# A hybrid decoder layer: modulation by pairs of feature tiles, with w_cond held in TensorE in float32

## The chip, the cores and the metric

The kernel runs on one core of a Trainium2 chip. The core has a matrix engine (TensorE, PE in the profile), three engines for elementwise work (VectorE or DVE, ScalarE or ACT, GpSimd or POOL), SyncE (SP), which issues most loads and stores, and 16 DMA engines that carry them. Every engine works through a queue of its own in a fixed order and waits for the others by semaphores. The metric is the device time of one execution in microseconds; less is better.

## The reference

One layer of a decoder with two branches, attention and a state-space model, on 1024 prompt tokens and 8 sample tokens. Only its first two steps matter here: the condition vector `c` of each of nine sequences (one prompt, eight samples) gives a shift and a scale for each of 1024 features, and the modulated input goes through one wide projection.

```python
def _modulate(x, c, w_cond, b_cond):
    mod = c @ w_cond + b_cond
    shift, scale, gate = jnp.split(mod, 3, axis=-1)
    h = x * (1.0 + scale[:, None]) + shift[:, None]
    return h, gate[:, None]

def _project_in(h, w_in):
    z = h @ w_in
    q, k, v, g_att, u, g_ssm, m_att, m_ssm = jnp.split(z, IN_SPLITS, axis=-1)
    ...
```

`c` is (1 + 8) x 1024, `w_cond` is 1024 x 3072 (the gate's third is used at the end of the kernel and is not touched here), `h` is 1032 x 1024, `w_in` is 1024 x 8192. All is float32.

## The kernel before

Features lie along the 128 partitions, so the transposed input `xt` comes as eight tiles of 128 features by 1032 tokens (`xs[t]`). Float32 products are made of faster ones: an operand is split into a high part (rounded, a cast on ScalarE) and a low part (the difference, on VectorE), and three products hi x hi, hi x lo, lo x hi are summed. For the projections the parts of a tile are `ahi` and `alo` (`split_act`), those of a slab of w_in (512 KB, 128 output features) `whi` and `wlo` (`Weights.emit`; one buffer for the slab as it comes, two for its parts).

A projection job (`gemm`) takes one slab and writes 128 output features in three column chunks: 8 feature tiles x 3 chunks x 3 products, 72 matmuls of 128x128 by 344 columns. The first four jobs are q, k, v and the gate of head pair 0. `Stream` hands out their matmuls: `begin` opens jobs, `head` takes matmuls of the opened ones ahead of time, `drain` and `weave` run the rest, the latter between the steps of the attention.

`modulate` (L241) runs at the very start. For the first half of the features (tiles 0 to 3), then for the second, it forms rows of `mod`: `c`, split and packed into 128 columns (`csplit`), is held in TensorE, and the split w_cond (`wchi`, `wclo`, in pieces of 256 rows by 512 columns, 16 loads in all) moves past it (`cond_product`, L346). The result, 9 rows of high and 9 of low parts, is copied out (`modr`, L270), and `features` (L277) turns it into columns by 8 small matmuls with a selector `sel`, in float32, of 128 columns held and 9 moving (each float32 matmul of the program stands as two in the trace: 16 there). Then `md` gets the bias (L281, L282), each tile is modulated, tiles 1, 3, 5, 7 on ScalarE (L285), 0, 2, 4, 6 on VectorE (L287), the sample columns by L288 and L289, and split (L236, L237). During the second half, `head(FILL)` puts five projection matmuls of jobs 0 and 1 behind each piece, up to half of each job.

The tables of the state-space model (`ssm_tables`, a generator that `modulate` advances by `next(tabs)`) are woven in: small loads (a_re, a_im, log_dt, mult), some 45 steps of 128x32 on VectorE (L383 to L413), four large steps on GpSimd (L418 to L427) with rounding steps on VectorE between them (L379, L425), two sines on ScalarE (L428, L429), and products. The order on VectorE, ScalarE, GpSimd and SyncE is set when the program is built, by a scheduler with priorities (`high_priority` moves a step ahead); on TensorE it is the order in which the code is written.

After job 0, the q columns are copied (`Attention.evac`, L581), split on ScalarE (L586) and GpSimd (L587); after job 1 the k columns likewise, their parts are turned to the other half of the partitions by DMAs (L612, L614), and the first scores (L661) multiply them.

Of the kernel before, what the change touches and what calls it, by code (L numbers as in the profile page):

```python
# [9 lines left out]
F32 = mybir.dt.float32  # L10
F32R = mybir.dt.float32r
I32 = mybir.dt.int32
AF = mybir.ActivationFunctionType
ALU = mybir.AluOpType
# [3 lines left out]
NP, NS, NT = 1024, 8, 1032  # L18
NC3, CW = 3, 344
KT = 8  # L20
# [11 lines left out]
EDGE = 2  # L32
ORDER = {3: (3, 0, 1, 2), 0: (0,), 2: (0, 2, 1), 1: (1, 0)}
HURRY = 400
WCB = 8
ONACT = (1, 3, 5, 7)
FILL = 5
WQ = "pps"
QUEUES = "sasssasss"
PACE = 155  # L40
# [2 lines left out]
GS = "v"  # L43
LATE = 5.0
AHEAD = 2
FILL2 = 10
DRAIN = 1.6
EARLY = 2
TWO_PI = 6.283185307179586
MULT = [float(j) for j in range(9)] + [8.0 * j for j in range(16)] + [128.0 * j for j in range(8)]  # L50
NM = len(MULT)
# [33 lines left out]
def blk(i, w=128):  # L85
    return slice(w * i, w * i + w)
# [61 lines left out]
class Stream:  # L148
# [24 lines left out]
    def head(self, n):  # L173

        for job in self.begun:
            while n and job[1] < KT * 9 // 2:
                next(job[0])
                job[1] += 1
                n -= 1
                self.left -= MM  # L180
                self.clock += MM

# [59 lines left out]
def modulate(k, sp, ps, io, tabs):  # L242


    nc, S = k.nc, k.stream
    PE, ACT, DVE, SP = nc.tensor, nc.scalar, nc.vector, nc.sync
    ct = sp.tile([128, KT, 9], F32, name="ct", bufs=1)
    SP.dma_start(ct, io["ct"])
    cc = split_c(k, sp, ct)
    todo = deque((q, 1024 * s + 512 * half) for half in range(2) for s in range(2) for q in range(4))  # L250
    ahead, xs = deque(), {}

    def load():
        if todo:
            q, c0 = todo.popleft()
            ahead.append(cond_load(k, sp, io, q, c0, WCB))

    def load_x(half):
        for t in range(4 * half, 4 * half + 4):
            xs[t] = sp.tile([128, NT], F32, tag="xt", bufs=5, name="xt")  # L260
            SP.dma_start(xs[t], io["xt"][t])

    def rows(fill):
        ps_ = ps.tile([128, 512], F32, tag="mod", name="mod")
        for q in range(4):
            cond_product(k, ps_, cc, q, cond_split(k, sp, ahead.popleft(), 2))
            load()
            fill()
        r = sp.tile([64, 512], F32, tag="modr", bufs=2, name="modr")
        ACT.copy(r, ps_[0:64])  # L270
        return r

    def features(half, rs):
        pm = ps.tile([128, 512], F32, tag="mod", name="pm")[:, 0:128].rearrange("p (i s n) -> p i s n", i=4, s=2)
        for i in range(4):
            for s in range(2):
                PE.matmul(pm[:, i, s, 0:9], rs[s][:, blk(i)], sel, start=True, stop=True)  # L277
        for i in range(4):
            t = 4 * half + i
            md = sp.tile([128, 2, 9], F32, tag="md", bufs=2, name="md")  # L280
            DVE.tensor_scalar(md[:, 0], pm[:, i, 0, 0:9], bc[:, t:t + 1], None, op0=ALU.add)  # L281
            DVE.tensor_scalar(md[:, 1], pm[:, i, 1, 0:9], bc[:, 8 + t:9 + t], 1.0, op0=ALU.add, op1=ALU.add)  # L282
            x = xs.pop(t)
            if t in ONACT:
                ACT.activation(x[:, 0:NP], x[:, 0:NP], AF.Identity, scale=md[:, 1, 0:1], bias=md[:, 0, 0:1])  # L285
            else:
                DVE.tensor_scalar(x[:, 0:NP], x[:, 0:NP], md[:, 1, 0:1], md[:, 0, 0:1], op0=ALU.mult, op1=ALU.add)  # L287
            DVE.tensor_tensor(x[:, NP:NT], x[:, NP:NT], md[:, 1, 1:9], ALU.mult)  # L288
            DVE.tensor_tensor(x[:, NP:NT], x[:, NP:NT], md[:, 0, 1:9], ALU.add)  # L289
            k.act_h.append(split_act(k, k.hp, x))  # L290

    for n in range(WCB):
        if n == EARLY:
            next(tabs)
        load()
    sel = sp.tile([64, 9], F32, name="sel", bufs=1)
    SP.dma_start(sel, io["sel"])
    bc = sp.tile([128, 16], F32, name="bc", bufs=1)
    SP.dma_start(bc, io["bc"])
    next(tabs)  # L300
    load_x(0)
    k.w.ahead = 2
    k.w.ensure()
    SP.dma_start(k.ident, io["ident"])
    SP.dma_start(k.hb, io["sb_bias"].broadcast_to((128, H)))
    r = [rows(lambda: None) for _ in range(2)]
    features(0, r)
    load_x(1)
    k.w.ahead = 0
    S.begin(2)  # L310
    r = [rows(lambda: S.head(FILL)) for _ in range(2)]
    S.head(FILL2)
    features(1, r)
    S.head(72)
    k.w.ahead = 1


def split_c(k, sp, ct, tag="csplit"):

    nc = k.nc  # L320
    cc = sp.tile([128, KT, 128], F32R, name="csplit", tag=tag, bufs=1)
    nc.vector.memset(cc.bitcast(F32), 0.0)
    nc.vector.tensor_copy(cc[:, :, 0:9], ct)
    nc.vector.tensor_tensor(cc[:, :, 32:41], ct, cc[:, :, 0:9].bitcast(F32), ALU.subtract)
    return cc
# [1394 lines left out]
```

## Time and profile before

| what | value |
|---|---|
| median of 3 runs | 1667.35 us (1664.79 to 1669.0) |
| profiled execution | 1668.55 us, span 1666.5 us |
| TensorE busy | 1497.7 us, 90% of the span |
| VectorE busy | 1265.3 us, 76% |
| ScalarE busy | 754.0 us, 45% |
| GpSimd busy | 895.0 us, 54% |
| mean granted TensorE clock | 0.958 |

The span runs from the first to the last instruction; the execution's own time is about 2 us longer. Busy shares are means over stages that differ: the first 80 us are the modulation, the tables and the first two jobs, then come attention, the state-space branch and the output products. A time in the timeline is counted from the span's start; the second number of a row is the duration of one instruction or of a run of like ones, and a bracket tells the idle time ahead of it and what ended it.

### The profile page before, as it was taken

How to read it: one execution, taken by the hardware profiler on the slowest of the kernel's cores; microseconds unless marked ns; L12 is line 12 of the kernel's file. 1: busy time of each engine (PE TensorE's matmuls, PEld its weight loads, DVE VectorE, ACT ScalarE, POOL GpSimd, SP SyncE). 2: the span in 40 equal slices, each digit the busy share in tenths (PEclk: the TensorE clock that was granted, in tenths of full speed). 3: DMA queues.
4: the chain of work that ended last, by engine and by line, in shares of the span. 5: the costliest groups of instructions: out<-in, count | busy, mean ns of one | idle time of the engine just before them, and what ended most of it. 6: DMA issues, size and time to landing. Idle time of an engine off the chain costs nothing.

```text
span 1666.5 us, 26016 instructions
## 1 busy us (share of the span) xinstructions
PE 1497.7 (90%) x9257; PEld 1423.4 (85%) x9257; DVE 1265.3 (76%) x2342; ACT 754.0 (45%) x1380; POOL 895.0 (54%) x744
## 2 busy tenths in 40 slices
PE   4899899999999999999989898987988869999997
PEld 3799898989898989899978888887878869999885
DVE  8748888888888888872688878978559994544566
ACT  4466666666676666663333333333352222321200
POOL 3437676767676767664456555456336542122154
PEclk8899999999999999999999999889989989999998
DMA  9233333333333333326689888768355576754322
GB/s 333 71 100 82 81 81 81 81 81 81 82 81 82 81 81 81 81 88 205 214 274 292 261 256 266 256 200 233 113 181 172 188 266 240 250 182 150 105 89 89
DMA packets 164125, 258.72 MB, mean 155 GB/s; under 512 B 45049, under 2 KB 106233, under 8 KB 163867
## 3 DMA queue, kind: packets, MB, share of 16 engines
q1 hardware_dynamic: 137945, 163.62, 32.5%
q0 software_dynamic: 23456, 84.95, 15.9%
q10 hardware_dynamic: 2594, 8.49, 1.9%
q8 instruction: 73, 1.20, 0.3%
q14 instruction: 57, 0.47, 0.1%
HBM read 188.38 MB, written 57.86 MB: 148 GB/s over the span
## 4 chain that ended last, share of the span: by engine, by line
PE 41%; DVE 25%; issue 8%; DMA 5%; ACT 4%; POOL 2%; SPq 0%; DVEq 0%; ACTq 0%; POOLq 0%
PE pj L142 26%; PE f L1403 6%; DVE l_t L895 4%; DVE s_sc L837 3%; DVE ke L672 3%; PE o L707 3%; PE tp L690 2%; DMA s_t<-in_cache_k,s_idx 2%; PE z L661 2%; DVE vs L643 2%; DVE be L673 2%; DVE s_t L832 1%; DMA w<-in_w_in 1%; DVE m L1255 1%; DVE ox L716 1%
## 5 line engine op out<-in xcount | busy, mean ns | idle before, releaser
L142 PE MATMUL pj<-ahi,whi 128*128 128x344 f32 x2112 | 700.9, 333 | 56.9 <-ACT u L981 20.4
L142 PE MATMUL pj<-alo,whi 128*128 128x344 f32 x2112 | 691.3, 329 | 10.3 <-DVE alo L1231 5.8
L142 PE MATMUL pj<-ahi,wlo 128*128 128x344 f32 x2112 | 585.0, 329 | 14.2 <-POOL wlo L110 14.2
L142 PEld LDWEIGHTS pj<-ahi,whi 128*128 128x128 f32 x2112 | 410.3, 194 | 65.6 <-ACT u L981 21.4
L142 PEld LDWEIGHTS pj<-alo,whi 128*128 128x128 f32 x2112 | 410.5, 194 | 15.3 <-DVE alo L1231 6.9
L142 PEld LDWEIGHTS pj<-ahi,wlo 128*128 128x128 f32 x2112 | 385.0, 193 | 17.6 <-POOL wlo L110 15.8
L672 DVE TENSOR_TENSOR_SCAN ke<-ke,eye 128x896 f32<-128x896 f32 (+7 forms) x128 | 214.2, 1674 | 81.9 <-ACT ke L662 81.5
L110 POOL TENSOR_TENSOR wlo<-w,whi 128x1024 fp32r<-128x1024 f32 x53 | 134.2, 2532 | 242.7 <-ACT whi L109 242.4
L109 ACT CAST whi<-w 128x1024 fp32r<-128x1024 f32 x90 | 94.9, 1055 | 162.0 <-PE pj L142 111.3
L662 ACT ACTIVATE ke<-z,nhb 128x448 f32<-128x448 f32 (+2 forms) x192 | 112.0, 583 | 82.6 <-PE z L661 79.2
L673 DVE TENSOR_TENSOR be<-be,ke 128x896 f32<-128x896 f32 (+7 forms) x128 | 128.3, 1003 | 11.7 <-DVE ke L672 0.5
L837 DVE SCALAR_TENSOR_TENSOR s_sc<-s_t,s_q,s_sc 128x512 f32<-128x512 f32 x126 | 112.4, 892 | 22.0 <-issue 9.9
L663 ACT ACTIVATE be<-z,hb 128x448 f32<-128x448 f32 (+2 forms) x192 | 110.7, 577 | 0.0
L816 POOL DMA_INDIRECT s_t<-in_cache_k,s_idx x64 | 71.3, 1114 | 39.8 <-issue 12.8
L690 PE MATMUL tp<-ident,be 128*128 128x128 f32 x576 | 89.4, 273 | 0.0
L495 POOL TENSOR_TENSOR pr<-tab 128x256 f32<-128x256 f32 x32 | 31.1, 972 | 102.4 <-DMA tab<-d_tab 98.8
L693 ACT CAST wthi<-tp 128x512 fp32r<-128x512 f32 x96 | 56.6, 590 | 54.7 <-PE tp L690 52.6
L895 DVE SCALAR_TENSOR_TENSOR l_t<-l_t,l_sc 128x128 f32<-128x128 f32 x256 | 78.5, 366 | 2.3 <-DMA l_t<-in_cache_v,l_idx 2.3
L496 POOL TENSOR_TENSOR pt<-tab 128x256 f32<-128x256 f32 x64 | 77.8, 1216 | 3.1
L574 POOL TENSOR_TENSOR sg<-sg,zg 128x1024 f32<-128x1024 f32 x8 | 22.0, 2746 | 99.2 <-ACT sgs L573 99.2
L1525 ACT ACTIVATE gate<-pj 128x344 f32<-128x344 f32 x72 | 33.0, 459 | 92.2 <-PE pj L142 90.1
L661 PE MATMUL z<-kl,qs 128*128 128x448 f32 (+2 forms) x192 | 66.7, 348 | 3.0 <-DMA kl<-kl 3.0
(320 smaller groups left out, 2865.6 us busy)
## 6 DMA issues: line engine op xcount, KB each, us to landing
w<-in_w_in SPq DMA_DIRECT2D x38, 512.0 KB
w<-in_w_in POOLq DMA_DIRECT2D x26, 512.0 KB
wc<-in_w_cond SPq DMA_DIRECT2D x24, 512.0 KB
gst<-d_gg SPq DMA_DIRECT2D x8, 576.0 KB
x<-in_xr SPq DMA_DIRECT2D x9, 512.0 KB
xt<-in_xt SPq DMA_DIRECT2D x8, 516.0 KB
d_ma<-gate SPq DMA_DIRECT2D x8, 516.0 KB
d_mm<-gate SPq DMA_DIRECT2D x8, 516.0 KB
```

The source lines that it names most:

```text
L109: nc.scalar.copy(whi, w32)
L110: self.eng.tensor_tensor(wlo, w32, whi.bitcast(F32), ALU.subtract)
L142: PE.matmul(ps[c], w[:, blk(t)], x[:, cs(c)], start=(t == 0 and i == 0), stop=(t == KT - 1 and i == 2))
L661: nc.tensor.matmul(z[:, 0:wide], st["q", h][:, blk(i)], x[:, s:s + wide], start=j == 0, stop=j == 1)
L662: nc.scalar.activation(ke[:, s:s + cw], z[:, 0:cw], AF.Sigmoid, bias=k.nhb[:, hd:hd + 1], scale=-0.125)
L663: nc.scalar.activation(be[:, s:s + cw], z[:, 0:cw], AF.Sigmoid, bias=k.hb[:, hd:hd + 1], scale=0.125)
L672: nc.vector.tensor_tensor_scan(rev, rev, self.eye[:, NP - n:][:, ::-1], 0.0, ALU.mult, ALU.add)
L673: nc.vector.tensor_tensor(be, be, ke[:, 1:n + 1], ALU.mult)
L690: PE.transpose(tp[:, 2 * order[a] + e], w[e][:, blk(2 * j + a)], k.ident)
L837: DVE.scalar_tensor_tensor(sc, t, q[:, d - d0:d - d0 + 1], sc, op0=ALU.mult, op1=ALU.add)
L895: nc.vector.scalar_tensor_tensor(t[:, d], t[:, d], 1.0, self.sc, op0=ALU.mult, op1=ALU.mult, accum_out=self.acc[:, j, 8 * c + d:8 * c + d ...
L1403: PE.matmul(pp[c], a[:, token(i)], w[:, blk(c, 512)], start=(t == 0 and a is ah and w is wh), stop=(t == KT - 1 and a is al))
```

## The change

Modulation goes by pairs of feature tiles, four of them. w_cond comes in blocks of 512 rows by 256 columns (1 KB rows), four for a pair, and is held in TensorE unsplit, in float32; `c` moves past it with its 9 columns, also unsplit. The product of a pair stands in features by columns at once (`pm`), so `sel`, `csplit`, `wchi`, `wclo` and `modr` go. One VectorE step adds both biases for a pair (`bcs`, with the 1 of 1 + scale in it). All eight tiles are modulated on ScalarE. `head(n)` now brings each opened job up to its n-th matmul: after the small matmuls of pair g, jobs 0 and 1 follow up to 18 g, that is through tiles 0 to 2 g - 1, two tiles behind. The loads are ordered pair by pair, with the first slab of w_in behind pair 0 and the second among those of pair 3; the tables' small loads come behind pair 1.

```diff
 EDGE = 2
 ORDER = {3: (3, 0, 1, 2), 0: (0,), 2: (0, 2, 1), 1: (1, 0)}
 HURRY = 400
-WCB = 8
-ONACT = (1, 3, 5, 7)
-FILL = 5
+WCB = 12
+XTB = 6
 WQ = "pps"
 QUEUES = "sasssasss"
 PACE = 155
...
 GS = "v"
 LATE = 5.0
 AHEAD = 2
-FILL2 = 10
 DRAIN = 1.6
-EARLY = 2
 TWO_PI = 6.283185307179586
 MULT = [float(j) for j in range(9)] + [8.0 * j for j in range(16)] + [128.0 * j for j in range(8)]
 NM = len(MULT)
...
     def head(self, n):
 
         for job in self.begun:
-            while n and job[1] < KT * 9 // 2:
+            while job[1] < n:
                 next(job[0])
                 job[1] += 1
-                n -= 1
                 self.left -= MM
                 self.clock += MM
 
...
     PE, ACT, DVE, SP = nc.tensor, nc.scalar, nc.vector, nc.sync
     ct = sp.tile([128, KT, 9], F32, name="ct", bufs=1)
     SP.dma_start(ct, io["ct"])
-    cc = split_c(k, sp, ct)
-    todo = deque((q, 1024 * s + 512 * half) for half in range(2) for s in range(2) for q in range(4))
-    ahead, xs = deque(), {}
-
-    def load():
-        if todo:
-            q, c0 = todo.popleft()
-            ahead.append(cond_load(k, sp, io, q, c0, WCB))
-
-    def load_x(half):
-        for t in range(4 * half, 4 * half + 4):
-            xs[t] = sp.tile([128, NT], F32, tag="xt", bufs=5, name="xt")
+    ws, xs = {}, {}
+
+    def load(g):
+        for s in range(2):
+            for half in range(2):
+                w = ws[s, half, g] = sp.tile([128, 4, 256], F32, tag="wc", bufs=WCB, name="wc")
+                c0 = 1024 * s + 256 * g
+                SP.dma_start(w, io["w_cond"][512 * half:512 * half + 512, c0:c0 + 256].rearrange("(t p) f -> p t f",
+                                                                                                 p=128))
+        for t in (2 * g, 2 * g + 1):
+            xs[t] = sp.tile([128, NT], F32, tag="xt", bufs=XTB, name="xt")
             SP.dma_start(xs[t], io["xt"][t])
 
-    def rows(fill):
-        ps_ = ps.tile([128, 512], F32, tag="mod", name="mod")
-        for q in range(4):
-            cond_product(k, ps_, cc, q, cond_split(k, sp, ahead.popleft(), 2))
-            load()
-            fill()
-        r = sp.tile([64, 512], F32, tag="modr", bufs=2, name="modr")
-        ACT.copy(r, ps_[0:64])
-        return r
-
-    def features(half, rs):
-        pm = ps.tile([128, 512], F32, tag="mod", name="pm")[:, 0:128].rearrange("p (i s n) -> p i s n", i=4, s=2)
-        for i in range(4):
-            for s in range(2):
-                PE.matmul(pm[:, i, s, 0:9], rs[s][:, blk(i)], sel, start=True, stop=True)
-        for i in range(4):
-            t = 4 * half + i
-            md = sp.tile([128, 2, 9], F32, tag="md", bufs=2, name="md")
-            DVE.tensor_scalar(md[:, 0], pm[:, i, 0, 0:9], bc[:, t:t + 1], None, op0=ALU.add)
-            DVE.tensor_scalar(md[:, 1], pm[:, i, 1, 0:9], bc[:, 8 + t:9 + t], 1.0, op0=ALU.add, op1=ALU.add)
-            x = xs.pop(t)
-            if t in ONACT:
-                ACT.activation(x[:, 0:NP], x[:, 0:NP], AF.Identity, scale=md[:, 1, 0:1], bias=md[:, 0, 0:1])
-            else:
-                DVE.tensor_scalar(x[:, 0:NP], x[:, 0:NP], md[:, 1, 0:1], md[:, 0, 0:1], op0=ALU.mult, op1=ALU.add)
-            DVE.tensor_tensor(x[:, NP:NT], x[:, NP:NT], md[:, 1, 1:9], ALU.mult)
-            DVE.tensor_tensor(x[:, NP:NT], x[:, NP:NT], md[:, 0, 1:9], ALU.add)
+    def features(g):
+        pm = ps.tile([128, 512], F32, tag="mod", name="pm")[:, 0:36].rearrange("p (i s n) -> p i s n", i=2, s=2)
+        for s in range(2):
+            for i in range(2):
+                for t in range(KT):
+                    PE.matmul(pm[:, i, s], ws[s, t // 4, g][:, t % 4, blk(i)], ct[:, t], start=t == 0, stop=t == KT - 1)
+        md = sp.tile([128, 2, 2, 9], F32, tag="md", bufs=2, name="md")
+        with k.tc.high_priority(HURRY):
+            DVE.tensor_tensor(md, pm, bcs[:, 2 * g:2 * g + 2].unsqueeze(3).broadcast_to([128, 2, 2, 9]), ALU.add)
+        for i in range(2):
+            x = xs.pop(2 * g + i)
+            ACT.activation(x[:, 0:NP], x[:, 0:NP], AF.Identity, scale=md[:, i, 1, 0:1], bias=md[:, i, 0, 0:1])
+            DVE.tensor_tensor(x[:, NP:NT], x[:, NP:NT], md[:, i, 1, 1:9], ALU.mult)
+            DVE.tensor_tensor(x[:, NP:NT], x[:, NP:NT], md[:, i, 0, 1:9], ALU.add)
             k.act_h.append(split_act(k, k.hp, x))
 
-    for n in range(WCB):
-        if n == EARLY:
-            next(tabs)
-        load()
-    sel = sp.tile([64, 9], F32, name="sel", bufs=1)
-    SP.dma_start(sel, io["sel"])
+    load(0)
     bc = sp.tile([128, 16], F32, name="bc", bufs=1)
     SP.dma_start(bc, io["bc"])
-    next(tabs)
-    load_x(0)
+    bcs = sp.tile([128, KT, 2], F32, name="bcs", bufs=1)
+    DVE.tensor_copy(bcs[:, :, 0], bc[:, 0:KT])
+    DVE.tensor_scalar(bcs[:, :, 1], bc[:, KT:], 1.0, None, op0=ALU.add)
     k.w.ahead = 2
     k.w.ensure()
+    load(1)
+    next(tabs)
+    load(2)
     SP.dma_start(k.ident, io["ident"])
     SP.dma_start(k.hb, io["sb_bias"].broadcast_to((128, H)))
-    r = [rows(lambda: None) for _ in range(2)]
-    features(0, r)
-    load_x(1)
+    features(0)
+    load(3)
     k.w.ahead = 0
     S.begin(2)
-    r = [rows(lambda: S.head(FILL)) for _ in range(2)]
-    S.head(FILL2)
-    features(1, r)
-    S.head(72)
+    for g in range(1, 4):
+        features(g)
+        S.head(18 * g)
+        if g == 1:
+            next(tabs)
     k.w.ahead = 1
```

In the rows of the order below, L numbers are lines of the kernel that the row is from (the lines of after are 3 to 19 less), `x` counts like rows, `pj` is a projection, `mod` the old product, `pm` the small products.

TensorE at the start of the program. Before, in the stretch of the first to the second half:

```order
L346 MATMUL mod<-wchi,csplit 128x512
L346 MATMUL mod<-wclo,csplit 128x512
L346 MATMUL mod<-wchi,csplit 128x512
L346 MATMUL mod<-wclo,csplit 128x512
L277 MATMUL pm<-sel,modr 128x9 x8
L346 MATMUL mod<-wchi,csplit 128x512
L346 MATMUL mod<-wclo,csplit 128x512
L346 MATMUL mod<-wchi,csplit 128x512
L346 MATMUL mod<-wclo,csplit 128x512
L142 MATMUL pj<-ahi,whi 128x344
L142 MATMUL pj<-alo,whi 128x344
L142 MATMUL pj<-ahi,wlo 128x344
```

After, from the small matmuls of pairs 0 and 1 on:

```order
L263 MATMUL pm<-ct,wc 128x9 x64
L139 MATMUL pj<-ahi,whi 128x344
L139 MATMUL pj<-alo,whi 128x344
L139 MATMUL pj<-ahi,wlo 128x344
L139 MATMUL pj<-ahi,whi 128x344
L139 MATMUL pj<-alo,whi 128x344
L139 MATMUL pj<-ahi,wlo 128x344
```

and around those of pair 2, with the end of job 1's first 18 ahead of them:

```order
L139 MATMUL pj<-alo,whi 128x344
L139 MATMUL pj<-ahi,wlo 128x344
L139 MATMUL pj<-ahi,whi 128x344
L139 MATMUL pj<-alo,whi 128x344
L139 MATMUL pj<-ahi,wlo 128x344
L263 MATMUL pm<-ct,wc 128x9 x32
L139 MATMUL pj<-ahi,whi 128x344
L139 MATMUL pj<-alo,whi 128x344
L139 MATMUL pj<-ahi,whi 128x344
L139 MATMUL pj<-alo,whi 128x344
L139 MATMUL pj<-ahi,whi 128x344
L139 MATMUL pj<-alo,whi 128x344
```

The small matmuls of pairs 0 and 1 now stand at the very start, those of pairs 2 and 3 between blocks of 36 projections, the first block 18 of job 0 and 18 of job 1; the old products with five projections each are gone.

VectorE, around the tables' last small steps and the parts of tiles and slabs (`sm`, `t_mg`, `tf`, `tt` are the tables'). Before:

```order
L379 TENSOR_SCALAR tt<-tf 128x1056
L110 TENSOR_TENSOR wlo<-w_242,whi 128x1024
L289 TENSOR_TENSOR xt<-xt,md 128x8
L434 TENSOR_TENSOR t_mg<-t_mg,sm_145 128x32
L289 TENSOR_TENSOR xt<-xt,md 128x8
L237 TENSOR_TENSOR alo<-xt,ahi 128x1032 x2
L338 TENSOR_TENSOR wclo<-wc,wchi 128x1024 x2
L237 TENSOR_TENSOR alo<-xt,ahi 128x1032
L379 TENSOR_SCALAR tt<-tf 128x1056
L237 TENSOR_TENSOR alo<-xt,ahi 128x1032
L338 TENSOR_TENSOR wclo<-wc,wchi 128x1024
```

After:

```order
L373 SCALAR_TENSOR_TENSOR sm_328<-sm_352,sm_353 128x32
L1542 TENSOR_SCALAR nhb<-hb 128x16
L415 TENSOR_TENSOR t_mg<-t_mg,sm_328 128x32 x2
L266 TENSOR_TENSOR md<-pm,bcs 128x36
L415 TENSOR_TENSOR t_mg<-t_mg,sm_328 128x32
L270 TENSOR_TENSOR xt<-xt,md 128x8 x2
L415 TENSOR_TENSOR t_mg<-t_mg,sm_328 128x32
L271 TENSOR_TENSOR xt<-xt,md 128x8 x2
L415 TENSOR_TENSOR t_mg<-t_mg,sm_328 128x32 x4
L360 TENSOR_SCALAR tt<-tf 128x1056
L233 TENSOR_TENSOR alo<-xt,ahi 128x1032 x2
L107 TENSOR_TENSOR wlo<-w_132,whi 128x1024
```

`md` of pair 1 stands behind the tables' `t_mg`, and the low parts of tiles 2 and 3 and of the second slab behind one another; the old low parts `wclo` are gone from between.

ScalarE, around the two sines (`tf`, `tg`). Before:

```order
L337 CAST wchi<-wc 128x1024 x2
L428 ACT_TABLE_LOAD
L428 ACTIVATE tf<-tf 128x1056
L337 CAST wchi<-wc 128x1024 x2
L109 CAST whi<-w_248 128x1024
L270 COPY modr<-mod 64x512
L337 CAST wchi<-wc 128x1024 x2
L429 ACTIVATE tg<-tg 128x1056
L270 COPY modr<-mod 64x512
```

After:

```order
L269 ACTIVATE xt<-xt,md 128x1024 x2
L232 CAST ahi<-xt 128x1032 x2
L106 CAST whi<-w_132 128x1024
L409 ACT_TABLE_LOAD
L409 ACTIVATE tf<-tf 128x1056
L410 ACTIVATE tg<-tg 128x1056
L269 ACTIVATE xt<-xt,md 128x1024 x2
L232 CAST ahi<-xt 128x1032 x2
L269 ACTIVATE xt<-xt,md 128x1024 x2
```

Both sines now stand between the cast of the second slab and the modulation of tiles 4 and 5; before, they stood among the casts of w_cond in the second half.

## Rows read from the trace of the kernel before

**Rows 1.** Stretches: busy time (count) by engine, PEclk, DMA share, GB/s.

```profile
20.00:40.00 20.00, 5.94 (x27) 4.18 (x26) 19.90 (x57) 9.68 (x11) 12.07 (x4) 0.66 1.03 382
```

**Rows 2.** Waits, 0 to 100 us: total, times, longest.

```profile
PEld mod L346 <- DVE wclo L338: 16.9, 9, 5.3
```

**Rows 3.** Timeline, 79 to 98 us, two engines: start, duration, instruction, idle before.

```profile
79.51 1.05 ACT L109 CAST whi<-w 128x1024 fp32r<-128x1024 f32 x1 [3.87 <-PE pj L142]
...
97.14 0.44 PE L661 MATMUL z<-kl,qs 128*128 128x448 f32 x1 [3.04 <-DMA kl<-kl]
```

**Rows 4.** Timeline of ScalarE, 0 to 11 us: casts that wait for loads.

```profile
5.18 1.04 ACT L337 CAST wchi<-wc 128x1024 fp32r<-128x1024 f32 x1 [3.08 <-DMA wc<-in_w_cond]
...
10.18 1.04 ACT L337 CAST wchi<-wc 128x1024 fp32r<-128x1024 f32 x1 [2.56 <-DMA wc<-in_w_cond]
```

**Rows 5.** Timeline of ScalarE, 28 to 32 us: modulation and casts.

```profile
28.01 1.24 ACT L285 ACTIVATE xt<-xt,md 128x1024 f32<-128x1024 f32 x1 [5.45 <-DVE md L282]
...
30.09 2.00 ACT L236 CAST ahi<-xt 128x1032 fp32r<-128x1032 f32 x2
```

**Rows 6.** Timelines of VectorE, then GpSimd, 20 to 42 us.

```profile
20.84 0.17 DVE L379 TENSOR_SCALAR sm<-sm 128x32 f32<-128x32 f32 x1
...
22.89 0.17 DVE L413 TENSOR_SCALAR sm<-sm 128x32 f32<-128x32 f32 x1
...
27.24 0.22 DVE L281 TENSOR_SCALAR md<-pm,bc 128x9 f32<-128x9 f32 x1
...
35.16 2.37 DVE L237 TENSOR_TENSOR alo<-xt,ahi 128x1032 fp32r<-128x1032 f32 x2
...
23.06 2.00 POOL L421 TENSOR_TENSOR tg<-sm,mult 128x1056 f32<-128x1056 f32 x1 [22.53 <-DVE sm L413]
...
35.23 5.81 POOL L440 COPY tab<-t_mg 128x32 f32<-128x32 f32 x1 [0.22 <-DVE xt L289]
```

**Rows 7.** Timeline of TensorE at three places: products, small matmuls, transposes, projections.

```profile
8.13 0.63 PE L346 MATMUL mod<-wchi,csplit 128*128 128x512 f32 x1
8.56 0.63 PE L346 MATMUL mod<-wclo,csplit 128*128 128x512 f32 x1
...
64.66 1.95 PE L277 MATMUL pm<-sel,modr 64*128 64x9 f32 x16
...
84.05 0.32 PE L142 MATMUL pj<-ahi,wlo 128*128 128x344 f32 x1
84.21 0.32 PE L142 MATMUL pj<-ahi,whi 128*128 128x344 f32 x1
...
89.39 0.60 PE L632 MATMUL tp<-ident,z 128*128 128x128 f32 x4
89.74 0.41 PE L142 MATMUL pj<-ahi,whi 128*128 128x344 f32 x1
...
565.73 0.49 PE L142 MATMUL pj<-alo,whi 128*128 128x344 f32 x1
566.02 0.49 PE L142 MATMUL pj<-ahi,wlo 128*128 128x344 f32 x1
...
567.13 1.06 PE L632 MATMUL tp<-ident,z 128*128 128x128 f32 x4
567.84 0.64 PE L142 MATMUL pj<-alo,whi 128*128 128x344 f32 x1
```

**Rows 8.** Stretches of 2 and 3 us, columns as in rows 1.

```profile
7.00:9.00 2.00, 1.53 (x5) 1.18 (x5) 2.00 (x7) 0.61 (x1) 0.00 (x0) 1.00 0.64 187
63.00:66.00 3.00, 3.00 (x23) 2.79 (x23) 2.35 (x6) 0.00 (x0) 2.55 (x3) 1.00 0.00 0
66.00:69.00 3.00, 3.00 (x17) 2.98 (x17) 2.36 (x6) 1.25 (x1) 2.84 (x3) 0.72 0.00 0
92.00:95.00 3.00, 2.10 (x15) 1.75 (x13) 0.00 (x0) 1.37 (x2) 2.69 (x3) 1.00 0.97 264
566.00:568.00 2.00, 2.00 (x10) 1.94 (x10) 1.90 (x4) 0.92 (x2) 0.57 (x1) 0.50 0.75 166
```

## The prediction

> **What bounds the kernel now.** I read the stretches first. From 20 to 40 us TensorE is busy 5.94 us, at 0.66 of its clock, while VectorE is busy 19.90 us and the DMA share is full [rows 1]. So in this opening TensorE is the engine with room. The waits name what holds it: its weight loads for the old w_cond product stood 16.9 us behind VectorE's low parts `wclo` [rows 2]. The kernel pays for splitting w_cond, on a VectorE that also has the tables to do.
>
> The opening counts only by when it hands over. Job 0 (q of head pair 0) ends at 79.51, where TensorE lets go ScalarE's cast of the third slab; the copies, splits and turns of q and k follow, and the first score matmul starts at 97.14, after 3.04 us of idle TensorE [rows 3]. From the 145th projection matmul on, every engine's order is as before. So the change is worth what it does to the end of job 0, as long as that chain of 17.6 us follows it.
>
> **The change, part by part.** Gone are 16 casts, 16 subtractions `wclo`, 64 products, 32 selector matmuls and four row copies. Added are 128 float32 matmuls of 128x128 by 9 columns, 32 for each pair, and four of eight modulations go from VectorE to ScalarE. The loads keep their bytes.
>
> *What a small matmul costs.* The nearest row is the old selector product: 8 matmuls of the program, 16 in the trace, 1.95 us at full clock [rows 7, 8], so 0.244 us for each of the program's, with 9 columns moving as in the new ones. A pair's block of 32 is then 7.8 us. A matmul with so few columns must be paying for its weights, and the row for that at a low clock are the transposes, each with a weight load of its own: four start to next start 0.35 us at full clock (89.39 to 89.74), 0.71 us (567.13 to 567.84) in a stretch with a granted clock of 0.50 [rows 7, 8]. Weight loads double there, so I take a block at 1.2 GHz as 32 x 0.488 = 15.6 us.
>
> By the Trainium skill, "TensorE: Matmul & The Clock Gate", section "LDWEIGHTS (loading the stationary operand)", loading takes the held columns over 1.2 GHz, 107 ns for 128, with no term for the clock. By it a block of 64 loads would be an estimated 6.8 us at either level. The four transposes of 0.71 speak against it.
>
> *Which clock.* At the very start the clock column reads 1.00, but the products are 0.43 us apart (8.13 to 8.56): 0.84 ns a column, which is what projections of 344 columns take at 0.50 (0.29, 565.73 to 566.02) [rows 7, 8]. So TensorE starts at 1.2 GHz. And small matmuls don't keep 2.4: around the 16 of 64.66 TensorE was busy 3.00 of 3.00 us in both stretches, yet the clock went from 1.00 to 0.72 [rows 8], which means that some 1.3 us at full were followed by 1.7 at half. They began at 64.66; the fall was near 67.3, after 2.6 us. I take a block that begins at full clock as 2.6 us at full (11 matmuls), then 21 x 0.488, together 12.9.
>
> *Landing.* The first load is there at 5.1 [rows 4]. Half a megabyte at 382 GB/s [rows 1] takes 1.37 us; the first slab, the 7th load, lands at 13.3. The tables' inputs follow the 13th large load; between 5.18 and 10.18 [rows 4] lie 5.0 us where two loads take 2.7, so small inputs cost about 2.2, and the awaited one (log_dt) is there at 23 to 24. The second slab, the 22nd, lands near 36. w_cond's rows are 1 KB now, and no row has such a load: 1.37 is one bound, 1.98 the other (264 GB/s, where stores of 512 B rows ran beside a load [rows 8]). I take 1.37, nearer by tensor and direction.
>
> *To the second slab's parts.* Pairs 0 and 1 stand first in TensorE's queue, at 1.2 GHz: 5.1 to 20.7 to 36.3; their loads come sooner. `md` of pair 0 at 20.9, two activations of 1.24 and a cast of 1.0 [rows 5] give `ahi` of tile 0 at 24.4; VectorE has both low parts at 26.8 (1.19 each [rows 6]). Then 44 table steps: 20 started 0.11 apart (20.84 to 22.89), dependent ones more, so 0.12 x 44 = 5.3, to 32.1. GpSimd starts there as it did at 23.06, and `md` came 4.2 later, at 27.24 [rows 6]; in the new order too `md` of pair 1 stands behind these steps: 36.3. Both chains meet at 36.4. Two activations and two casts, 4.4, end at 40.8; `alo` of tile 2 can start at 39.8, and three subtractions (tiles 2 and 3, `wlo` of the slab) end at 43.4, or a GpSimd step of 2.00 later [rows 6] if one gets between; a GpSimd copy of 32 elements took 5.81 while VectorE ran on [rows 6], so mostly VectorE goes first. With the small rounding steps between, I take 45.
>
> *TensorE from there.* All else stands behind job 1's first 18 projections, which need that `wlo`. A projection starts every 0.16 us at full clock (84.05 to 84.21), every 0.29 at half [rows 7]. 18 after a long wait: 2.8 to 5.2, I take 12 slow and 6 fast, 4.4. Block of pair 2: 7.8 to 15.6, taken as 12.9. 36 projections: 5.7 to 10.4, 11 of them slow, 7.1. Pair 3 the same, 12.9 and 7.1. The last 18 of job 0: 2.8. Sum 4.4 + 40 + 2.8 = 47.2, so job 0 ends at 92.2. The modulation of tiles 4 to 7 (2 activations, 2 casts and a subtraction, 5.7 behind each `md`) lies beside 36 projections of 7.1; that cover is gone only if those run at full clock throughout.
>
> *Sum.* 92.2 - 79.5 = 12.7 later. Of the 17.6 us behind it a little comes back: job 1 now ends 2.8 behind job 0 where it was 5.8, and ScalarE and VectorE are past their early load; at most 3, I take 1.5. The profiled execution of 1668.55 (span 1666.5) becomes 1679.7; the runs' median, 1667.35, becomes 1678.5, say **1678**.
>
> **The rivals.** *The clock holds.* If small matmuls neither let it fall nor slow with it, pairs 0 and 1 leave the front to the tables (log_dt at 23, `md` of pair 1 at 34, parts at 42 to 44), and TensorE needs 4.4 + 2 x (7.8 + 7.1) + 2.8 = 37: job 0 ends at 80, the kernel at 1666 to 1668. Against it: 0.72 [rows 8] and the doubled transposes. For it: no row has a float32 matmul of 9 columns at half clock.
>
> *Faster: everything at 2.4 GHz.* The parts at 42.1, and projections at 0.16 throughout: 2.8 + 2 x (7.8 + 5.7) + 2.8 = 32.6, job 0 ends at 74.7, 4.8 sooner, with the 1.5 behind it 6.3: 1661. It decides from a TensorE sum under 35 (at 42.1 + 35 the gain is under 4). For it: 16.9 us of waits do go [rows 2]. Against it: the start at 0.43, which alone puts pairs 0 and 1 until 36.
>
> *All at 1.2 GHz.* 5.2 + 2 x (15.6 + 10.4) + 5.2 = 62.4, from 45: 107.4, 1694. For it: short stretches of 36 between blocks that let it fall. Against it: projections of before come back to 0.16 within a job.
>
> *1 KB rows at 1.98.* Eight w_cond loads stand ahead of log_dt: 5 us later there, which meets pair 1's chain at 36.4 and moves `md` to 41; 1682.
>
> *Given back later.* The attention behind may have slack for it, if another engine ends last there; TensorE is 90% busy, so I give it little.
>
> **How the numbers follow.** About 0.3%, 5.0 us, is what a measurement of this kernel tells from no change. Chances: the forecast, with the 1 KB rows in it, 0.61 (1672 to 1686), all at 1.2 GHz 0.11 (slower), the clock holds 0.16 (0.13 same, 0.03 slower), given back 0.04 (same at best 0.02, else slower), faster 0.08. So faster 0.08, same 0.15, slower 0.77. The range, 1664 to 1688, leaves out the faster case and the far part of all at 1.2 GHz.
>
> **What would show it.** In the changed kernel: 64 small matmuls in the trace for a pair, 0.24 apart at the start, the two blocks ending near 36; `md` of pair 1 there; `wlo` of the second slab at 45; blocks of 12 to 16 us later, with a granted clock near 0.5 in their second part; the third slab's cast, job 0's end, near 92; the first scores 16 to 17 us behind, and every later step shifted by one amount. It is wrong if a block takes 8 us or less in the second half, if job 0 ends under 84, or if the shift shrinks on the way.

## The result

The changed kernel takes 1675.87 us (median of 6 runs, 1671.36 to 1677.59) where the kernel before takes 1666.85 in the same comparison: a ratio of 1.006, 95% interval 1.0041 to 1.0078. So it is slower by 9 us, 0.6%. (One execution of the mix of small matmuls and projections below took 8152.52 us; the time given there is the median of the other three.) Its profiled execution took 1677.59 us, span 1675.9, against 1668.55 and 1666.5.

Timeline of TensorE after, up to the first scores (start, duration, instruction, idle before; `x128` counts like instructions, L263 are the small matmuls, L139 the projections):

```profile
5.50 27.45 PE L263 MATMUL pm<-ct,wc 128*128 128x9 f32 x128 [5.50 <-DMA wc<-in_w_cond]
32.80 0.63 PE L139 MATMUL pj<-ahi,whi 128*128 128x344 f32 x1
...
45.93 0.65 PE L139 MATMUL pj<-ahi,wlo 128*128 128x344 f32 x1 [4.32 <-DVE wlo L107]
...
49.95 11.35 PE L263 MATMUL pm<-ct,wc 128*128 128x9 f32 x64
61.16 0.63 PE L139 MATMUL pj<-ahi,whi 128*128 128x344 f32 x1
...
69.17 10.19 PE L263 MATMUL pm<-ct,wc 128*128 128x9 f32 x64
79.22 0.63 PE L139 MATMUL pj<-ahi,whi 128*128 128x344 f32 x1
...
86.77 0.32 PE L139 MATMUL pj<-ahi,whi 128*128 128x344 f32 x1
```

Pairs 0 and 1 take TensorE from 5.50 to 32.80. From 45.93 on it never stops: 4.0 us for the last 16 of job 1's first 18 projections, 11.2 for the small matmuls of pair 2, 8.0 for 36 projections, 10.1 for pair 3, 7.6 for 36 more, 2.8 for the last 18 of job 0. There is no wait left to blame in this stretch; it is TensorE's own work.

Where job 0 ends, and what follows, on ScalarE, GpSimd and TensorE:

```profile
89.64 1.05 ACT L106 CAST whi<-w 128x1024 fp32r<-128x1024 f32 x1 [0.33 <-PE pj L139]
92.47 4.87 POOL L568 TENSOR_TENSOR qs<-z,qs 64x1024 fp32r<-64x1024 f32 x2 [11.96 <-ACT qs L567]
97.41 5.71 POOL L594 TENSOR_TENSOR kl<-z,kh 64x1024 fp32r<-64x1024 f32 x2
...
107.16 0.71 PE L642 MATMUL z<-kl,qs 128*128 128x448 f32 x1 [5.04 <-DMA kl<-kl]
```

Job 0 ends at 89.64, where it ended at 79.51 [rows 3]: 10.1 us later. The first scores with `kl` follow 17.5 us behind, as before, at 107.16 instead of 97.14. From there the shift between these two traces stays about 10, wanders up to 14.5 (near 500 us) and is 9.3 from 1375 us to the end. So the loss of the opening is about what the kernel loses. But one trace tells this to some 5 us only: the changed kernel and the one with 36 columns below are level at 350 us and 5.3 us apart at the end.

Stretches of after: length, busy time (count) of PE, PEld, DVE, ACT, POOL, then PEclk, DMA share, GB/s:

```profile
10.00:20.00 10.00, 10.00 (x48) 10.00 (x49) 2.10 (x8) 1.48 (x2) 0.00 (x0) 1.00 1.07 370
20.00:40.00 20.00, 18.31 (x79) 17.87 (x79) 14.97 (x65) 8.07 (x9) 6.71 (x4) 1.00 1.00 343
51.00:52.00 1.00, 1.00 (x12) 1.00 (x11) 0.00 (x0) 0.00 (x0) 1.00 (x1) 1.00 0.00 0
52.00:53.00 1.00, 1.00 (x9) 1.00 (x9) 0.00 (x0) 0.00 (x0) 1.00 (x2) 0.74 0.00 0
53.00:54.00 1.00, 1.00 (x6) 1.00 (x6) 0.20 (x1) 0.96 (x1) 1.00 (x3) 0.50 0.00 0
```

Before, TensorE was busy 5.94 us of 20 to 40 [rows 1]; now it is 18.31. And in the middle of pair 2's block, with TensorE busy every moment, its granted clock falls from 1.00 to 0.50, and the small matmuls from 12 in a microsecond to 6.

### The profile page after: what moved, and what is told of

Same layout as the page of the kernel before. It is cut to its first block, busy times and chain, and to the rows that moved or that the text cites. A ratio compares the mean times of both kernels' runs of the same rounds, so it can differ in the third digit from the quotient of the medians.

```text
span 1675.9 us, 26246 instructions
## 1 busy us (share of the span) xinstructions
PE 1525.1 (91%) x9417; PEld 1459.8 (87%) x9417; DVE 1240.5 (74%) x2309; ACT 739.4 (44%) x1364; POOL 891.4 (53%) x744
## 4 chain that ended last, share of the span: by engine, by line
PE 49%; DVE 24%; issue 9%; DMA 7%; ACT 5%; POOL 4%; SPq 2%; DVEq 0%; POOLq 0%; ACTq 0%
PE pj L139 31%; PE f L1384 6%; DVE ke L653 4%; DVE l_t L876 4%; PE o L688 3%; PE tp L671 2%; PE pm L263 2%; PE z L642 2%; DVE vs L624 2%; DVE be L654 2%; DMA w<-in_w_in 2%; DVE s_sc L818 2%; DMA s_t<-in_cache_k,s_idx 1%; DVE ox L697 1%; DVE m L1236 1%
## 5 line engine op out<-in xcount | busy, mean ns | idle before, releaser
L139 PE MATMUL pj<-ahi,whi 128*128 128x344 f32 x2112 | 703.6, 335 | 53.7 <-ACT u L962 18.1
L139 PE MATMUL pj<-alo,whi 128*128 128x344 f32 x2112 | 693.1, 329 | 8.7 <-DVE alo L1212 5.8
L139 PE MATMUL pj<-ahi,wlo 128*128 128x344 f32 x2112 | 586.5, 330 | 17.5 <-POOL wlo L107 13.2
L139 PEld LDWEIGHTS pj<-ahi,whi 128*128 128x128 f32 x2112 | 412.0, 195 | 63.0 <-ACT u L962 19.1
L139 PEld LDWEIGHTS pj<-alo,whi 128*128 128x128 f32 x2112 | 412.0, 195 | 12.6 <-DVE alo L1212 6.8
L139 PEld LDWEIGHTS pj<-ahi,wlo 128*128 128x128 f32 x2112 | 387.0, 194 | 20.8 <-POOL wlo L107 14.9
L818 DVE SCALAR_TENSOR_TENSOR s_sc<-s_t,s_q,s_sc 128x512 f32<-128x512 f32 x126 | 107.5, 853 | 21.9 <-DMA s_t<-in_cache_k,s_idx 15.3
L797 POOL DMA_INDIRECT s_t<-in_cache_k,s_idx x64 | 71.1, 1111 | 38.7 <-issue 12.6
L477 POOL TENSOR_TENSOR pt<-tab 128x256 f32<-128x256 f32 x64 | 74.2, 1159 | 3.1
```

The lines of the kernel that those rows point to most:

```text
L139: PE.matmul(ps[c], w[:, blk(t)], x[:, cs(c)], start=(t == 0 and i == 0), stop=(t == KT - 1 and i == 2))
L818: DVE.scalar_tensor_tensor(sc, t, q[:, d - d0:d - d0 + 1], sc, op0=ALU.mult, op1=ALU.add)
```

## The experiments

**Theory:** job 0 is late because the float32 small matmuls take TensorE's time, two weight loads each and most of them at 1.2 GHz, and everything else stands behind them. **Rivals:** what is late is the start at 45.93 (loads, tables, low parts), or the loads in 1 KB rows. Each experiment is one edit of the changed kernel; a time without an interval is a single execution. On the chips of these runs the kernel before took 1663.6 to 1664.8 us (medians), not 1667, so a time is to be judged by its ratio to that kernel.

### Half of the small matmuls of pairs 2 and 3

```diff
-                for t in range(KT):
+                n = KT if g < 2 else KT // 2
+                for t in range(n):
...
```

> The changed kernel, with half of the small matmuls of pairs 2 and 3 left out (only the first four of eight feature tiles of c are summed there). Theory (TensorE's own time in the small matmuls after 46 us makes job 0 late): their two blocks, 11.2 and 10.1 us in the changed kernel, fall to 4 to 5 us each, job 0 ends 11 to 13 us earlier (77 to 79), and the kernel takes 1663 to 1666. Rival (the late parts of the second slab at 45.9, or a wait in the modulation of tiles 4 to 7, set the end): the blocks get shorter but the projections behind them wait for ScalarE or VectorE instead, job 0 ends at 85 or later, and the time stays above 1671.

Measured: 1660.57 us (before, on this chip: 1663.87).

```profile
50.12 3.94 PE L264 MATMUL pm<-ct,wc 128*128 128x9 f32 x32
60.95 4.47 PE L264 MATMUL pm<-ct,wc 128*128 128x9 f32 x32
...
76.21 1.05 ACT L106 CAST whi<-w 128x1024 fp32r<-128x1024 f32 x1 [0.33 <-PE pj L139]
```

TensorE and, last, ScalarE at job 0's end, which comes a little sooner than expected. The first block starts where it did (50.12), so nothing ahead of it moved; two blocks shorter by 13 us end job 0 13.4 us sooner. The projections behind them didn't wait for another engine. That is the theory, and against the rival: in this stretch TensorE's own work sets the end.

### Thirty-six columns moving instead of nine

```diff
-                    PE.matmul(pm[:, i, s], ws[s, t // 4, g][:, t % 4, blk(i)], ct[:, t], ...
+                    PE.matmul(pm[:, i, s], ws[s, t // 4, g][:, t % 4, blk(i)], ct4[:, t], ...
```

> The changed kernel, with 36 columns moving in each small matmul instead of 9 (c four times over; three copies are not used). Theory (the price is the weight load; columns cost nothing beside it): pairs 0 and 1 take 27 to 28 us again, the blocks of pairs 2 and 3 10 to 11.5 us each, the clock falls in them as before, time within 2 us of the changed kernel. Rival (the price is in the moving columns): each instruction gets longer by 27 columns of 0.4 to 1.7 ns, 0.01 to 0.05 us at full clock and twice that at half: blocks of 12 to 17 us, job 0 later by 3 to 12 us.

Measured: 1672.22 us (before, on this chip: 1663.87); job 0 ends at 88.94.

```profile
5.06 27.49 PE L266 MATMUL pm<-ct,wc 128*128 128x36 f32 x128 [5.06 <-DMA wc<-in_w_cond]
50.29 10.59 PE L266 MATMUL pm<-ct,wc 128*128 128x36 f32 x64
68.44 10.51 PE L266 MATMUL pm<-ct,wc 128*128 128x36 f32 x64
```

Four times the columns cost nothing: 27.49 against 27.45, 10.59 and 10.51 against 11.35 and 10.19. The price is not in what moves. That it lies in the weight load is the remaining reading, and it is not shown: the kernel that was to test it, with operands in the one-pass form of the projections and so half as many instructions, gave no time.

### A hundred and twenty-six columns moving

The same edit with c fourteen times over.

> The changed kernel with 126 columns moving in each small matmul instead of 9 (c fourteen times over; thirteen copies are not used), the order unchanged. Theory (it is the low clock that makes the small matmuls and the projections behind them dear; columns lie beside the weight load): with this much moving, TensorE comes to 2.4 GHz within pairs 0 and 1 (18 to 24 us instead of 27.4) and holds it; the blocks of pairs 2 and 3 take 7.8 to 9 us each instead of 11.2 and 10.1, and the 36 projections behind them 5.7 each instead of 8.0 and 7.6; job 0 ends 7 to 10 us sooner, at 79 to 83, and the kernel takes 1666 to 1669. Rival (the low price is not the clock's, or columns cost): each instruction takes 0.05 to 0.1 us longer for its 117 more columns, job 0 ends 5 to 20 us later, 1680 to 1695.

Measured: 1659.67 us, ratio to the kernel before 0.998 (0.9964 to 0.9995). With fourteen times the columns the kernel is 0.2% faster than the one before, where the changed kernel is 0.6% slower: some 13 us between the two. The time and job 0's end are better than expected.

```profile
5.36 11.00 PE L266 MATMUL pm<-ctn,wc 128*128 128x126 f32 x72 [5.36 <-DMA wc<-in_w_cond]
16.71 6.52 PE L266 MATMUL pm<-ctn,wc 128*128 128x126 f32 x56 [0.35 <-DMA wc<-in_w_cond]
...
47.68 7.55 PE L266 MATMUL pm<-ctn,wc 128*128 128x126 f32 x64
54.99 0.40 PE L139 MATMUL pj<-ahi,whi 128*128 128x344 f32 x1
...
60.76 7.30 PE L266 MATMUL pm<-ctn,wc 128*128 128x126 f32 x64
67.82 0.41 PE L139 MATMUL pj<-ahi,whi 128*128 128x344 f32 x1
...
76.46 1.05 ACT L106 CAST whi<-w 128x1024 fp32r<-128x1024 f32 x1 [0.33 <-PE pj L139]
```

The stretch that holds both blocks' ends, columns as above:

```profile
50.00:60.00 10.00, 10.00 (x79) 10.00 (x79) 4.11 (x12) 5.64 (x6) 7.69 (x7) 1.00 0.01 2
60.00:70.00 10.00, 10.00 (x84) 10.00 (x83) 2.38 (x11) 1.67 (x2) 5.73 (x6) 1.00 0.27 111
```

Pairs 0 and 1 are done at 23 us instead of 32.8: their last 56 instructions take 6.52 us, 0.12 each, where nine columns took 0.214. So the clock rose there already. The granted clock stays at 1.00 through both later blocks. They take 7.3 and 7.1 us to the next projection instead of 11.2 and 10.1; the 36 projections between them 5.8 instead of 8.0; those behind pair 3, to job 0's end, 8.6 instead of 10.4. That is 3.9 + 3.0 + 2.2 + 1.8 = 10.9 us by the clock. Job 0 ends at 76.46, 13.2 sooner; the other 2.3 come from pair 2's block starting at 47.68: VectorE's order near the tables came out differently here (`md` of pair 1 at 24.42, ahead of most of them), and the second slab's parts were ready at 42.93. So of the 21 us that the two blocks take in the changed kernel, and the 4 by which the projections behind them are slow, about 11 are the low clock that the small matmuls themselves bring about.

### Pair 2 ahead of the projections

```diff
-    for g in range(1, 4):
-        features(g)
-        S.head(18 * g)
-        if g == 1:
-            next(tabs)
+    features(1)
+    features(2)
+    S.head(18)
+    next(tabs)
+    S.head(36)
+    features(3)
+    S.head(54)
```

> The changed kernel with the small matmuls of pair 2 ahead of the first projections, right behind those of pairs 0 and 1. Theory: their 13 us at the lower clock run from 33 to 46.5, where TensorE otherwise had 5 us of projections and 8 us of idle time; the 36 projections follow (7 to 8 us), 36 more, pair 3 (10 to 11), 36 and 18: job 0 ends at 79 to 83 instead of 89.6, and the kernel takes 1666 to 1669, about the time before. Rival (the shift comes from elsewhere, from the loads or from ScalarE and VectorE): job 0 ends within 3 us of 89.6.

Measured: 1665.88 us, ratio to before 1.0019 (1.0002 to 1.0036).

```profile
5.27 41.10 PE L263 MATMUL pm<-ct,wc 128*128 128x9 f32 x192 [5.27 <-DMA wc<-in_w_cond]
...
80.00 1.05 ACT L106 CAST whi<-w 128x1024 fp32r<-128x1024 f32 x1 [0.33 <-PE pj L139]
```

Pair 2's matmuls, now at 1.2 GHz from first to last (192 at 0.214 us), cost 13.7 us of TensorE and yet job 0 ends 9.6 us sooner: they fill the time in which TensorE had waited for the second slab. So job 0's lateness is a matter of where the work stands, and the loads and the modulation bear this order. Not all of the time comes back: the first scores come at 97.24, where they came before, and yet the kernel takes 0.2%, some 3 us, more than the one before. Why is not settled.

### The second slab early

```diff
-    k.w.ahead = 2
+    k.w.ahead = 1
     k.w.ensure()
     load(1)
+    k.w.ahead, k.w.w32 = 2, sp.tile([128, KT * 128], F32, name="w32b", bufs=1)
+    k.w.ensure()
+    k.w.w32 = None
```

> The changed kernel with the second slab of w_in loaded right behind pair 1 into a buffer of its own, and so split ahead of tiles 2 and 3; the small matmuls stay where they are. Theory: job 1's first 18 follow job 0's without the idle 7.6 us (37.8 to 45.9 but for two matmuls) and pair 2's block starts at 42 instead of 50; all behind it moves by 6 to 8, job 0 ends at 81 to 84, 1668 to 1670. Rival (the second slab is only one of several steps that end near 46: the parts of tiles 2 and 3, or the tables ahead of the modulation of tiles 4 and 5): the gain is 3 us or less.

Measured: 1665.09 us, ratio to before 1.0017 (1.0002 to 1.0033).

```profile
40.50 10.19 PE L266 MATMUL pm<-ct,wc 128*128 128x9 f32 x64
...
78.62 1.05 ACT L109 CAST whi<-w 128x1024 fp32r<-128x1024 f32 x1 [0.33 <-PE pj L142]
```

Pair 2's block starts at 40.50 instead of 49.95, and job 0 ends 11.0 us sooner, more than expected. So the first rival has its part: the wait for the second slab, whose last piece is the 4.32 us ahead of 45.93 in the timeline above, is worth as much to job 0's end as the clock. Both are true: TensorE's line from 45.93 on is full, and it starts late. Here, too, the first scores (96.01) come no later than before, and the kernel takes 0.2% more: the time follows the first scores to some 4 us only.

### Small matmuls one by one among projections

```diff
                     PE.matmul(pm[:, i, s], ...
+                    n += 1
+                    if among:
+                        among(n)
...
+    features(2, lambda n: step(0, min(n, 18)))
+    next(tabs)
+    features(3, lambda n: step(1, min(n, 18)) if n <= 18 else S.head(18 + n - 18))
+    S.head(36)
+    S.head(54)
```

`step(j, n)` brings job j up to its n-th projection.

> The changed kernel with the small matmuls of pair 2 put one by one among job 0's first 18 projections and behind them, those of pair 3 among job 1's first 18 and the next 28. Theory: pair 2 runs where TensorE was idle (38 to 46), and projections of 344 columns between small matmuls keep the clock up, so pair 3's 64 cost 8 to 10 us; job 0 ends at 75 to 79, the kernel takes 1661 to 1665. Rival (small matmuls pull the clock down in the mix too): the mixed stretch goes at 1.2 GHz throughout, job 0 ends at 82 to 87, 1668 to 1673.

Measured: 1673.53 us, ratio to before 1.0069 (1.0049 to 1.009); job 0 ends at 90.13. The same with the second slab early:

> Both: the second slab early, pair 2's small matmuls among the first 18 projections of jobs 0 and 1, pair 3's among the next 36. Theory: from 33 us on TensorE has 144 projections and 128 instructions of small matmuls, 23 us and 16 at full clock, 4 to 6 more for the first ones at 1.2 GHz: job 0 ends at 74 to 77, 1659 to 1663, ahead of the kernel before. Rival (VectorE and GpSimd, who share the tables and the low parts between 36 and 60 us, set the end once TensorE doesn't): waits of 3 to 8 us for low parts of tiles 4 to 7 appear, job 0 ends at 78 to 82, 1664 to 1668.

Measured: 1673.90 us, ratio 1.0079 (1.0062 to 1.0097); job 0 ends at 90.27. The theory fell in both: the mix went at 1.2 GHz throughout, as the first rival said, and job 0 ended later than even that rival had it. The second rival fell too: TensorE did not wait. TensorE in the first of them, and the stretch around it:

```profile
60.39 0.43 PE L264 MATMUL pm<-ct,wc 128*128 128x9 f32 x2
60.67 0.63 PE L139 MATMUL pj<-ahi,whi 128*128 128x344 f32 x1
61.11 0.43 PE L264 MATMUL pm<-ct,wc 128*128 128x9 f32 x2
...
60.00:70.00 10.00, 10.00 (x43) 10.00 (x43) 2.72 (x2) 0.00 (x0) 6.09 (x4) 1.00 0.32 133
```

One float32 matmul and one projection go every 0.71 us: 0.43 + 0.28, the price of both at 1.2 GHz. At these prices TensorE goes on without a gap from 33 us to 82, through 14 small matmuls by themselves (from 45.9) and, later, one among every two projections. I had thought that wide projections in between would hold the clock up; it was low when the mix began, and the mix never brought it up. The clock column reads 1.00 here, and in the first 38 us of the changed kernel, though the spacing is that of 1.2 GHz: it seems to show 1.00 until the first change of level. There the spacing is to be trusted.

### All that helped, together

126 columns with the second slab early:

> 126 columns moving and the second slab early, small matmuls where the changed kernel has them. Theory (both gains, 10 us by the clock and 9 to 11 by the slab, come from different stretches): pairs 0 and 1 are done at 24, both first 18 by 33, pair 2's block by 42, and then the tables on VectorE and GpSimd (pair 3's modulation behind them) become the limit; job 0 ends at 66 to 74 and the kernel takes 1649 to 1658. Rival (the two gains are one and the same, the wait at 43 to 46): job 0 ends at 74 to 78, 1657 to 1661, as with 126 columns alone.

Measured: 1660.46 us, ratio to before 0.9986 (0.9971 to 1.0001), not to be told from the kernel before. Job 0 ends at 66.95, as expected; the time is not what was expected. With the mix as well:

> 126 columns, the second slab early, and small matmuls of pairs 2 and 3 one by one among projections. Theory (at 126 columns the mix costs nothing and fills what would be idle): like the kernel with blocks or up to 3 us sooner, job 0 at 64 to 74, 1647 to 1658. Rival (in a mix every switch between small matmuls and projections costs, 0.71 us for a pair of instructions and a projection at 1.2 GHz where the blocks' prices give 0.40 + 0.29): the mix is later by 1 to 4 us, and if the clock is low there, by 10 or more.

Measured: 1657.01 us, ratio 0.9966 (0.995 to 0.9982); job 0 ends at 68.86, both as expected. The mix of 126 columns begins at 0.71 us for a matmul and a projection (28.25 to 28.96) and goes at 0.38 from 30.37 on, so it brings the clock up, which that of 9 columns did not; 0.38 is the price of both at full clock, 0.22 + 0.16, and the mix itself costs nothing. ScalarE behind job 0's end, in the first, and TensorE's first scores:

```profile
66.95 1.05 ACT L109 CAST whi<-w 128x1024 fp32r<-128x1024 f32 x1 [6.30 <-PE pj L142]
73.25 1.04 ACT L109 CAST whi<-w 128x1024 fp32r<-128x1024 f32 x1 [5.25 <-DMA w<-in_w_in]
74.32 2.19 ACT L571 COPY z<-pj 128x344 f32<-128x344 f32 x6
...
91.31 0.71 PE L651 MATMUL z<-kl,qs 128*128 128x448 f32 x1 [4.22 <-DMA kl<-kl]
```

Job 0 ends 12.6 us before that of the kernel before, the first scores come only 5.8 sooner. ScalarE's queue now has the cast of the fourth slab ahead of the copies of q, and it waits 5.25 us for that slab's load; most of the 6.7 us that are lost on the way go there. With the three edits it is the same (5.18). So, with the third slab in a buffer of its own too, that the fourth may be loaded early:

> The kernel with all three edits (126 columns, second slab early, small matmuls among projections), and the third slab of w_in loaded into a buffer of its own during the modulation, so that the fourth, too, is loaded before job 0 ends. In the kernel with the three edits ScalarE stood 5.2 us for the fourth slab's load ahead of the copies of q, with 7.3 us between job 0's end (68.9) and those copies. Theory (that wait is where the gain between job 0's end and the first scores went): the copies start 3 to 4.5 us after job 0's end, the first scores 3 to 4 us sooner, at 88 to 90, and the kernel takes 1652 to 1655. Rival (the tables' last steps on VectorE and GpSimd, or the low parts of the slabs, are late next): the copies start sooner but the first scores stay at 92 to 93, 1657.

Measured: 1656.72 us, ratio 0.9953 (0.9932 to 0.9974).

```profile
72.04 1.04 ACT L109 CAST whi<-w 128x1024 fp32r<-128x1024 f32 x1 [1.86 <-PE pj L142]
73.11 2.19 ACT L596 COPY z<-pj 128x344 f32<-128x344 f32 x6
...
89.29 0.44 PE L676 MATMUL z<-kl,qs 128*128 128x448 f32 x1 [4.02 <-DMA kl<-kl]
```

The wait for the load is gone and the first scores come at 89.29 instead of 92.66, as expected; the time is the rival's, and the whole kernel gains nothing that can be told from 1657.01. In the two traces its lead of 4.5 us over the kernel with three edits is 1.8 at 600 us, and 1.7 behind at the end. Against the trace of the kernel before, the lead is 12.5 us at 1182 and 9 at 1342 in this profile, 12.6 and 11.9 in the other, so part of it is given back near 1200 us. Why, I did not settle, and it is within what traces differ by in these stages. These two are the fastest kernels of this study, 0.3 to 0.5% ahead of the kernel before.

## Why the prediction was right

The forecast was 1678, slower, by an end of job 0 at 92.2; it came at 89.64 and 1675.87. Step by step:

**What bounds, and the handover: right.** The opening counts by job 0's end, and the 17.6 us behind it [rows 3] are 17.5 now (forecast 16.1, see below).

**What a small matmul costs: right in kind, a tenth too high.** I took 0.244 us for each of the program's at full clock [rows 7], and twice that at 1.2 GHz, from the transposes. TensorE alone in pair 3's block, while the clock was up (length, busy time and count, PEclk, DMA share, GB/s; a count takes in what reaches over an edge):

```profile
69.30:70.30 1.00, 1.00 (x12) 1.00 0.18 26
...
69.30:72.30 3.00, 3.00 (x30) 1.00 0.06 9
...
72.00:73.00 1.00, 1.00 (x11) 0.98 0.00 0
73.00:74.00 1.00, 1.00 (x7) 0.50 0.00 0
```

Two microseconds more hold 18 instructions more: 0.11 each, 0.22 for each of the program's. At 1.2 GHz the 128 of pairs 0 and 1 took 27.45 us: 0.214 each, 0.43. So the price doubles nearly (1.9 times), and both levels are a tenth under what I took. (Part of that tenth was my reading of the row: the old 16 took 1.95 us with the end of the last, but 1.87 from the first start to the next matmul's.) By the Trainium skill, "TensorE: Matmul & The Clock Gate", section "LDWEIGHTS (loading the stationary operand)", a load takes its columns over 1.2 GHz, without a term for the clock; two loads of 128 columns would be an estimated 0.21 us at either level. The trace agrees at full clock (0.22) and not at the low one (0.43).

**Which clock: right.** TensorE starts at 1.2 GHz, and the small matmuls let the clock fall in both later blocks (0.74 in the stretch from 52 and 0.50 behind it; 0.98 from 72 and 0.50 behind it). The projections behind them went on slowly longer than I took: 8.0 and 7.6 us for 36 instead of 7.1.

**The front: right for a reason that I had only half.** `md` of pair 1 was forecast at 36.4 from two chains that meet. VectorE, then GpSimd, after:

```profile
31.40 1.91 DVE L373 SCALAR_TENSOR_TENSOR sm<-sm,sm 128x32 f32<-128x32 f32 x1
33.61 1.65 DVE L1542 TENSOR_SCALAR nhb<-hb 128x16 f32<-128x16 f32 x1 [0.29 <-DMA hb<-in_sb_bias]
...
35.54 0.18 DVE L266 TENSOR_TENSOR md<-pm,bcs 128x36 f32<-128x36 f32 x1
...
39.11 5.63 DVE L233 TENSOR_TENSOR alo<-xt,ahi 128x1032 fp32r<-128x1032 f32 x2 [1.31 <-ACT ahi L232]
44.67 1.21 DVE L107 TENSOR_TENSOR wlo<-w,whi 128x1024 fp32r<-128x1024 f32 x1
...
31.27 2.00 POOL L402 TENSOR_TENSOR tg<-sm,mult 128x1056 f32<-128x1056 f32 x1 [30.74 <-DVE sm L394]
33.22 2.01 POOL L399 TENSOR_TENSOR tf<-sm,mult 128x1056 f32<-128x1056 f32 x1
...
37.88 2.42 POOL L401 TENSOR_TENSOR tf<-tf,tt 128x1056 f32<-128x1056 f32 x1
40.37 3.28 POOL L403 TENSOR_TENSOR tf<-tf,tg 128x1056 f32<-128x1056 f32 x1
```

TensorE was done with pair 1 at 32.80; `md` came at 35.54, behind the steps ahead of it on VectorE, so that queue alone set it. Two of them were long: the last `sm` took 1.91 us, where the same step had taken 0.19 at 28.16, and `nhb`, which is not the tables', 1.65, where it took 0.17 in the kernel before. GpSimd's first two steps ran beside them. Then two low parts took 5.63 us instead of 2.4, while GpSimd's steps of 2.42 and 3.28 us ran: the step that I had said might get between did. My "mostly VectorE goes first" was wrong, and the trace of the kernel before had a row against it: a VectorE step of 8 columns that took 2.40 us at 32.64, beside a GpSimd step of 3.35. With these the second slab's low part is ready at 45.88, forecast 45: `md` was 0.8 early and the steps behind it 1.6 longer than I took, so that the nearness is partly luck.

**1 KB rows: near the bound taken.** 370 GB/s from 10 to 20 us and 343 from 20 to 40, against 382 [rows 1]: 1.42 to 1.53 us for half a megabyte, not 1.98. No wait of this stretch ends at a w_cond load but the first.

**The sum from there: 43.7 us, forecast 47.2.** 4.0 (4.4), 11.2 (12.9), 8.0 (7.1), 10.1 (12.9), 7.6 (7.1), 2.8 (2.8). (The first term is for 18 projections, of which two ran ahead, at 41.) The term that was mis-sized is the block, by 4.5 us in the two: the price of an instruction, a tenth too high, and in pair 3's the clock, which stayed up to 73, nearly 4 us after the block began, where I had taken 2.6. The 36 projections behind each, 1.4 us longer in the two, took part of that back.

**The 1.5 us that were to come back: wrong.** Job 1 does end sooner behind job 0, but GpSimd's parts of q and k stand in one queue, 4.87 and 5.71 us from 92.47 on; k's earlier end finds it busy. The errors, 3.5 us in the sum and the other way 0.9 in the front and 1.4 here, made the time come out nearer than its steps: that is luck, though the largest is under half of the 9 us.

**The rivals.** "The clock holds" is what 126 columns did in the two later blocks and behind them, and job 0's end (76.5) lies between that rival's 80 and the 74.7 of its faster neighbour, "everything at 2.4 GHz". The time does as well: 0.2% under the kernel before, where the two had it level and 0.4% under. "All at 1.2 GHz" is what the mix did in TensorE up to 82 us, but without idle time, so that job 0 ended at 90 and not at 107. "Given back later" did not come: the traces are 9.3 us apart at the end.

## What to carry to other kernels

Count a float32 matmul by what the trace shows for it, here two instructions of 0.11 us at full clock and 0.21 at 1.2 GHz, and count it at the clock that it will leave behind: replacing few wide products by many narrow ones can take the wait off one engine and put more than that on TensorE. When TensorE's line is full behind a late operand, look first at what can be moved into the wait ahead of it; two edits of the order here each brought job 0's end back to about where it had been, and some two thirds of the time with it. And when an opening gets shorter, follow the gain to the next handover: 5 us of 12.6 were lost here to one load for which a queue stood waiting.

## What was not expected of the hardware

Columns were free and more: 9 and 36 moving columns cost the same within 1 us in all three stretches, and 126 cost 0.11 us an instruction at full clock (64 in 7.1 us), as 9 did; but only the 126 kept the clock at 1.00; doing fourteen times the arithmetic made the kernel some 13 us faster. A mix of float32 small matmuls of 9 columns and projections of 344, busy without a gap, stayed at 1.2 GHz for 45 us; with 126 columns it began at that level and came up (0.71 us for a matmul and a projection at 28.25, 0.38 from 30.37 on). Two VectorE steps that take under 0.2 us elsewhere took 1.91 and 1.65 beside GpSimd's steps. The clock's column reads 1.00 from the start of a profile while spacing shows half.
